# Column sums for norms: rows or squares added on VectorE and one product with ones per chunk

## The chip, the cores and the metric

The kernel runs on one core of a Trainium2 chip. The metric is the device time of one execution in microseconds. A core has TensorE (PE; its weight loads are shown apart as PEld), VectorE (DVE), ScalarE (ACT), GpSimd (POOL), SyncE (SP) and DMA queues. Each engine works through its instructions in order; they wait for each other by semaphores.

## What is computed

Two blocks of a transformer-like network, one after the other, on 1024 tokens of 1024 features (the first with 16 more meta tokens, the second with a context of 256 tokens beside). The change touches only the sums over features that the norms need. In short:

```
# block 1
h = concat(meta, x)
p = rmsnorm(h, g) @ w_in                    # state-space mixer (s5) and gated recurrence (hgrn)
merged = sigmoid(.) * (y_a @ w_a) + sigmoid(.) * (y_b @ w_b)
h = h + merged @ w_out
z = rmsnorm(h, ffn_norm_g)                  # "merge" ends with this norm
u = causal_dwconv(z @ w_up)
h = h + (silu(u1) * u2) @ w_down
x = rmsnorm(h, final_norm_g)                # "ffn" ends with this norm
# block 2, first mixer (ab), for the context and for x
ctx = layer_norm(ALPHA * ctx + gate_c * ab_mixer(ctx), g, b)      # "context path"
x   = layer_norm(ALPHA * x + gate * ab_mixer(x), g, b)            # "ab_x"
# block 2, second mixer (cd: Fourier mixing and attention)
x   = layer_norm(ALPHA * x + gate * cd_mixer(x, ctx), g, b)       # "cd"

rmsnorm(x)    = x * rsqrt(mean(x * x) + EPS) * g
layer_norm(x) = (x - mean(x)) * rsqrt(mean((x - mean(x))^2) + EPS) * g + b
```

## The kernel before

Features lie on partitions, tokens on columns. So an activation of 1024 features is eight row tiles of 128 partitions, and a sum over features is a sum over partitions and over eight tiles. Tokens are worked on in three chunks, of 384, 256 and 384 columns (384, 384 and 258 in merge, 256 alone in the context path). A weight product is exact in fp32 to the accuracy wanted: weights and activations are split into two parts, and `mm3` (line 83) issues three products for each 128 x 128 block. In ffn's down projection they are at line 949. In the trace such a product is one record; an fp32 product with ones, which goes through the array in two passes, is two.

A stage that ends in a norm is written with `closing` (line 754): the first panels (128 output features each) go through all chunks, the last `nres` (3 in merge, 6 in ab_x, 7 in cd) chunk by chunk, so that the norm of one chunk can run beside the weight products of the next. The rows of the first panels are added up in one tile `acc` on VectorE. For the last panels, the sum over partitions goes through TensorE. Merge (`sq=True`) issues full-width products with a matrix of ones (lines 779 and 792), accumulating in one bank. The others call `col_sum` (line 800): four sources at a time go through 32 columns of ones each, side by side in the array, into four groups of 32 output partitions (line 813); ScalarE copies the four partial sums out (line 817), and one more product with a selection matrix adds them up in every partition (line 818). `tail` sources skip this and go straight into that last bank (line 808).

`ln_chunk` (line 1038) is the layer norm of a chunk: mean (line 1042), centring of the eight rows (line 1045), squares on ScalarE (line 1047), their `col_sum`, `rsqrt` (lines 106 to 111), and `emit`, which scales the rows and makes the next stage's input. Ffn's last group of products (lines 957 to 965) squares each finished row on ScalarE (line 963) and sums with `col_sum`; then `x1_chunk` (line 977) norms. The context path (line 1221) sums eight rows, then calls `ln_chunk`.

The order of instructions on each engine isn't the order of the code: a scheduler of the framework places them by its own estimate when what they read is ready. Weight products' banks (`mm`) are four, banks of the sums (`sm`) four.

## Time and profile before

| | |
|---|---|
| time, median of 3 runs | 3249.68 us (3247.68 to 3250.23) |
| span of the profiled execution, first to last instruction | 3242.6 us |
| the profiled execution's own time | not listed apart; the median is 7.1 us above the span |
| mean granted TensorE clock | 0.995 |
| TensorE busy | 3165.4 us, 98% |
| VectorE busy | 1831.4 us, 56% |
| ScalarE busy | 1126.1 us, 35% |

Busy shares are means over the whole span. Where the kernel waits is read from the timelines of the engines, the windows (busy time of each engine in a stretch) and the waits. The five stages are found at about 966 to 979 us (context path), 1340 to 1392 (merge), 2096 to 2153 (ffn), 2451 to 2518 (ab_x) and 3130 to 3218 us (cd). In a timeline, consecutive instructions of one kind are one row; the square brackets hold the idle time before it and what ended that.

### The profile page before, as it was taken

How to read it: one execution, taken by the hardware profiler on the slowest of the kernel's cores; microseconds unless marked ns; L12 is line 12 of the kernel's file. 1: busy time of each engine (PE TensorE's matmuls, PEld its weight loads, DVE VectorE, ACT ScalarE, POOL GpSimd, SP SyncE). 2: the span in 40 equal slices, each digit the busy share in tenths (PEclk: the TensorE clock that was granted, in tenths of full speed). 3: DMA queues.
4: the chain of work that ended last, by engine and by line, in shares of the span. 5: the costliest groups of instructions: out<-in, count | busy, mean ns of one | idle time of the engine just before them, and what ended most of it. 6: DMA issues, size and time to landing. Idle time of an engine off the chain costs nothing.

```text
span 3242.6 us, 47786 instructions
## 1 busy us (share of the span) xinstructions
PE 3165.4 (98%) x19986; PEld 2840.8 (88%) x19986; DVE 1831.4 (56%) x3508; ACT 1126.1 (35%) x1846; POOL 92.9 (3%) x99
## 2 busy tenths in 40 slices
PE   8999899999999999999999999999999999999998
PEld 6999887879999999999999999989997889555476
DVE  7549468775454334465554555455336464777744
ACT  5341733233344312232222222252224353544532
POOL 0000000000210000000000000000000000121100
PEclk9999999999999999999999999999999999999999
DMA  4342454343552234111111111111111223000211
GB/s 153 90 161 91 148 182 142 118 153 103 158 155 81 91 118 130 33 59 46 40 46 53 47 52 40 53 35 54 46 40 66 92 88 130 29 7 7 79 49 52
DMA packets 106384, 269.01 MB, mean 83 GB/s; under 512 B 14798, under 2 KB 43694, under 8 KB 105974
## 3 DMA queue, kind: packets, MB, share of 16 engines
q1 hardware_dynamic: 99656, 245.35, 23.3%
q10 hardware_dynamic: 4464, 16.34, 1.3%
q0 software_dynamic: 2048, 4.26, 0.7%
q8 instruction: 157, 2.57, 0.3%
q14 instruction: 59, 0.48, 0.0%
HBM read 219.12 MB, written 46.11 MB: 82 GB/s over the span
## 4 chain that ended last, share of the span: by engine, by line
PE 90%; DVE 4%; DMA 2%; ACT 2%; issue 1%; SPq 0%; DVEq 0%; ACTq 0%
PE mm L83 62%; PE mm L949 7%; PE sm L1558 4%; PE mm L1555 4%; PE sm L813 2%; PE mm L1124 2%; PE sm L1531 1%; DMA YBd<-o 1%; PE mm L1516 1%; ACT Tt L502 1%; DVE R L604 1%; PE sm L465 1%; PE sm L1573 0%; PE sm L708 0%; PE sm L1017 0%
## 5 line engine op out<-in xcount | busy, mean ns | idle before, releaser
L83 PE MATMUL mm<-z,whl 128*128 128x256 f32 (+3 forms) x4032 | 682.9, 325 | 1.5 <-ACT z L231 1.0
L83 PE MATMUL mm<-a,whl 128*128 128x384 f32 (+1 forms) x4320 | 682.7, 319 | 1.6 <-ACT u L917 1.6
L83 PEld LDWEIGHTS mm<-a,whl 128*128 128x128 f32 x4320 | 678.5, 188 | 3.7 <-ACT u L917 1.9
L83 PEld LDWEIGHTS mm<-z,whl 128*128 128x128 f32 x4032 | 637.6, 189 | 36.8 <-issue 29.2
L76 DVE TENSOR_TENSOR whl<-wraw,whl 128x1024 fp32r<-128x1024 f32 (+2 forms) x258 | 302.6, 1178 | 221.1 <-ACT whl L75 220.3
L75 ACT CAST whl<-wraw 128x1024 fp32r<-128x1024 f32 (+2 forms) x258 | 260.6, 1014 | 341.8 <-PE mm L949 137.0
L83 PE MATMUL mm<-hx,whl 128*128 128x384 f32 (+1 forms) x2232 | 366.3, 322 | 7.7 <-ACT fx L1378 7.1
L83 PEld LDWEIGHTS mm<-hx,whl 128*128 128x128 f32 x2232 | 352.0, 189 | 16.8 <-ACT fx L1378 7.3
L949 PE MATMUL mm<-g,whl 128*128 128x384 f32 (+1 forms) x1584 | 257.9, 322 | 2.3 <-DVE f L951 1.2
L949 PEld LDWEIGHTS mm<-g,whl 128*128 128x128 f32 x1584 | 248.0, 188 | 13.9 <-issue 8.1
L83 PE MATMUL mm<-b,whl 128*128 128x384 f32 (+1 forms) x1152 | 180.9, 319 | 0.0
L83 PEld LDWEIGHTS mm<-b,whl 128*128 128x128 f32 x1152 | 180.8, 189 | 0.0
L917 ACT COPY u<-mm 128x384 f32<-128x384 f32 x132 | 58.3, 445 | 317.8 <-PE mm L83 317.8
L951 DVE TENSOR_TENSOR f<-f,mm 128x384 f32<-128x384 f32 (+1 forms) x240 | 118.3, 508 | 71.3 <-PE mm L949 70.4
L1556 ACT ACTIVATE P<-mm 128x512 f32<-128x512 f32 x160 | 94.7, 597 | 134.4 <-PE mm L1555 127.9
L83 PEld LDWEIGHTS mm<-y,whl 128*128 128x128 f32 x816 | 120.2, 188 | 13.1 <-issue 9.8
L83 PE MATMUL mm<-y,whl 128*128 128x256 f32 (+1 forms) x816 | 128.1, 312 | 1.4 <-ACT y L741 1.1
L1558 PE MATMUL sm<-P,m 128*64 128x512 f32 x320 | 128.0, 611 | 0.6 <-ACT P L1556 0.5
L1532 DVE TENSOR_REDUCE mx<-sm 128x1 f32<-128x512 f32 (+1 forms) x192 | 105.7, 595 | 39.7 <-PE sm L1531 38.4
L1555 PE MATMUL mm<-m,KB 97*128 97x512 f32 x420 | 121.7, 405 | 0.0
L1555 PEld LDWEIGHTS mm<-m,KB 97*128 97x128 f32 x420 | 75.6, 188 | 47.4 <-issue 33.3
L923 DVE TENSOR_SCALAR av<-u,conv_w,conv_b 128x1024 f32<-128x1024 f32 x22 | 17.9, 812 | 138.7 <-ACT u L917 138.7
(519 smaller groups left out, 3664.0 us busy)
## 6 DMA issues: line engine op xcount, KB each, us to landing
wraw<-w_up SPq DMA_DIRECT2D x44, 512.0 KB, 3.2
wraw<-w_h SPq DMA_DIRECT2D x32, 512.0 KB, 3.4
wraw<-ab_w SPq DMA_DIRECT2D x32, 512.0 KB, 3.4
wm<-ab_w_mod SPq DMA_DIRECT2D x24, 512.0 KB
wm<-cd_w_mod SPq DMA_DIRECT2D x24, 512.0 KB, 4.0
wraw<-w_down SPq DMA_DIRECT2D x22, 512.0 KB, 3.2
ut<-Ud SPq DMA_DIRECT2D x16, 520.0 KB, 4.5
gt<-Gd SPq DMA_DIRECT2D x16, 513.0 KB, 3.2
```

The lines of the kernel that those rows point to most:

```text
L75: self.nc.scalar.copy(t[:, 0], raw)
L76: self.nc.vector.tensor_tensor(out=t[:, 1], in0=raw, in1=t[:, 0].bitcast(F32), op=ALU.subtract)
L83: nc.tensor.matmul(ps, W[:, wp, wofs + 128 * k:wofs + 128 * k + 128], X(xp, kofs + k, lo, hi), start=first and k == 0 and i == 0, stop=las ...
L813: nc.tensor.matmul(p4[32 * j:32 * j + 32], self.ones[:, 0:32], x, start=i < 4, stop=i - len(pend) + j + 5 >= m)
L917: return u, (self.split_w(A["w_up"][p], [1024]), lambda c, lo, hi, ps: nc.scalar.copy(u[:, lo:hi], ps))
L949: nc.tensor.matmul(ps, ws[j][:, wp, 128 * o:128 * o + 128], G[j][:, xp, lo:hi], start=n_ == 0 and i == 0, stop=n_ == len(js) - 1 and i == 2)
L951: v.tensor_tensor(out=h1[o][:, 2 + lo:2 + hi], in0=h1[o][:, 2 + lo:2 + hi], in1=ps, op=ALU.add)
L1124: nc.tensor.matmul(ps, X(xp, k, 128 * t, 128 * t + 128), wv[k // 4][:, wp, 256 * (k % 4):256 * (k % 4) + 256], start=k == 0 and i == 0, st ...
L1532: v.tensor_reduce(out=mx[:, qt, j:j + 1], in_=ps, axis=mybir.AxisListType.X, op=ALU.max)
L1555: nc.tensor.matmul(ps, K[0:97, kp, 128 * t:128 * t + 128], Q[0:97, qp, 512 * c:512 * c + 512], start=i == 0, stop=i == 2)
L1556: nc.scalar.activation(Pt[:, c], ps, AF.Exp, scale=scale)
L1558: nc.tensor.matmul(po[64 * c:64 * c + 64, :], vv(t)[:, 64 * h:64 * h + 64], Pt[:, c], start=t == 0, stop=t == KT - 1)
```

## The change

In 18 of the 23 column sums, the eight rows (or squares) of a chunk are added up on VectorE and go through one full-width product with ones. `closing` adds the last panels' rows, or for merge their squares, to `acc` as well; in the last chunk the last row goes through a product of its own into the same bank. Ffn adds its squares in `tot` in the same manner. `ln_chunk` adds the squares in the tile of the first one, except in the last chunk of a closing (`tail` 1), where `col_sum` stays. The context path adds its eight rows in the first tile of `sqs`, whose other three tiles then take the squares in turn. The sums of the opening norm stay as they are. By the order of instructions TensorE has 122 products fewer (of 18548), VectorE 107 instructions more, ScalarE 15 fewer. Removed comments make up the rest of the diff and are left out here.

```diff
@@ closing
         for c, (lo, hi) in enumerate(chunks):
             n = hi - lo
-            if sq:
-                pc = self.ps_sm()[:, 0:n]
-                nc.tensor.matmul(pc, self.ones, acc[:, lo:hi], start=True, stop=False)
-            else:
-                add = self.col_sum(nres + 1, n, lambda: tp.tile([128, 384], F32, tag="mu", name=self.nm("cse"), bufs=1), int(hi == chunks[-1][1]))
-                add(0, acc[:, lo:hi])
             for j, (w, o) in enumerate(ws):
...
                 if sq:
                     t = tp.tile([128, 384], F32, tag="tmp", name=self.nm("sqt"), bufs=2)[:, 0:n]
                     nc.scalar.activation(t, src, AF.Square)
-                    nc.tensor.matmul(pc, self.ones, t, start=False, stop=i == npan - 1)
-                else:
-                    pc = add(j + 1, src)
+                    src = t
+                if i == npan - 1 and hi == chunks[-1][1]:
+                    nc.tensor.matmul(pc, self.ones, src, start=False, stop=True)
+                    continue
+                nc.vector.tensor_tensor(out=acc[:, lo:hi], in0=acc[:, lo:hi], in1=src, op=ALU.add)
+                if i == npan - (2 if hi == chunks[-1][1] else 1):
+                    pc = self.ps_sm()[:, 0:n]
+                    nc.tensor.matmul(pc, self.ones, acc[:, lo:hi], start=True, stop=i == npan - 1)
             done(c, lo, hi, pc)
@@ ffn, last group
-                    add = self.col_sum(8, n, lambda: tp.tile([128, 384], F32, tag="cse", name=self.nm("cse"), bufs=1), int(c == 2))
+                    tot = tp.tile([128, 384], F32, tag="cse", name=self.nm("cse"), bufs=1)[:, 0:n]
                     for o in range(8):
                         one(o, lo, hi)
-                        t = tp.tile([128, 384], F32, tag="tmp", name=self.nm("sqt"), bufs=6)[:, 0:n]
+                        t = tp.tile([128, 384], F32, tag="tmp", name=self.nm("sqt"), bufs=6)[:, 0:n] if o else tot
                         nc.scalar.activation(t, h1[o][:, 2 + lo:2 + hi], AF.Square)
-                        pc = add(o, t)
+                        if o == 7 and c == 2:
+                            nc.tensor.matmul(pc, self.ones, t, start=False, stop=True)
+                            continue
+                        if o:
+                            v.tensor_tensor(out=tot, in0=tot, in1=t, op=ALU.add)
+                        if o == (6 if c == 2 else 7):
+                            pc = self.ps_sm()[:, 0:n]
+                            nc.tensor.matmul(pc, self.ones, tot, start=True, stop=o == 7)
@@ ln_chunk
-        add = self.col_sum(8, n, lambda: tp.tile([128, 384], F32, tag="mu", name=self.nm("cse"), bufs=1), tail)
+        if tail:
+            add = self.col_sum(8, n, lambda: tp.tile([128, 384], F32, tag="mu", name=self.nm("cse"), bufs=1), tail)
         for k in range(8):
             v.tensor_tensor(out=r(k), in0=r(k), in1=mu, op=ALU.subtract)
             t = sqt(k)[:, 0:n]
             nc.scalar.activation(t, r(k), AF.Square)
-            ps = add(k, t)
+            if tail:
+                ps = add(k, t)
+            elif k == 0:
+                t0 = t
+            else:
+                v.tensor_tensor(out=t0, in0=t0, in1=t, op=ALU.add)
+        if not tail:
+            ps = self.ps_sm()[:, 0:n]
+            nc.tensor.matmul(ps, self.ones, t0, start=True, stop=True)
@@ ctx_path
-            add = self.col_sum(8, T, lambda: tp.tile([128, 384], F32, tag="mu", name=self.nm("cse"), bufs=1))
-            for k in range(8):
-                ps = add(k, x[:, k])
             sqs = cp.tile([128, 4, T], F32, name="csq")
-            self.ln_chunk(tp, lambda k: x[:, k], ps, T, emit, lambda k: sqs[:, k % 4], 0)
+            tot = sqs[:, 0]
+            v.tensor_tensor(out=tot, in0=x[:, 0], in1=x[:, 1], op=ALU.add)
+            for k in range(2, 8):
+                v.tensor_tensor(out=tot, in0=tot, in1=x[:, k], op=ALU.add)
+            ps = self.ps_sm()[:, 0:T]
+            nc.tensor.matmul(ps, self.ones, tot, start=True, stop=True)
+            self.ln_chunk(tp, lambda k: x[:, k], ps, T, emit, lambda k: sqs[:, 1 + (k - 1) % 3 if k else 0], 0)
```

The order of instructions that results is shown at three places. The names are the output tile and what it is computed from, with the output's shape; x3 stands for three in a row.

TensorE, before, at the end of ffn's third chunk: `g` with `whl` are its weight products, `sqt` with `ones` the squares, `hx` the input of the next stage.

```order
L813 MATMUL sm_19587<-sqt_19671,ones 32x384
L813 MATMUL sm_19587<-sqt_19687,ones 32x384
L949 MATMUL mm_19711<-g_18997,whl_19191 128x384
L813 MATMUL sm_19587<-sqt_19703,ones 32x384
L949 MATMUL mm_19711<-g_18997,whl_19191 128x384
L949 MATMUL mm_19711<-g_19178,whl_19196 128x384 x3
L83 MATMUL mm_19808<-hx_19351,whl_19803 128x384 x2
L83 MATMUL mm_19834<-hx_19351,whl_19803 128x256
L818 MATMUL sm_19588<-cse_19708,sel 128x384
L83 MATMUL mm_19834<-hx_19351,whl_19803 128x256
L83 MATMUL mm_19808<-hx_19351,whl_19803 128x384
L808 MATMUL sm_19588<-sqt_19725,ones 128x384
```

TensorE, after, at the same place (`cse` is now the tile of the added squares):

```order
L950 MATMUL mm_19691<-g_18606,whl_19178 128x384 x3
L950 MATMUL mm_19691<-g_18989,whl_19183 128x384 x3
L950 MATMUL mm_19691<-g_19170,whl_19188 128x384 x3
L83 MATMUL mm_19788<-hx_19339,whl_19783 128x384
L972 MATMUL sm_19689<-cse_19571,ones 128x384
L966 MATMUL sm_19689<-sqt_19705,ones 128x384
L83 MATMUL mm_19788<-hx_19339,whl_19783 128x384 x2
L83 MATMUL mm_19788<-hx_19340,whl_19783 128x384 x3
```

Before, the narrow products of the squares stand among the weight products of the last rows; after, the two full products stand together, behind the last weight product and one product of the next stage.

VectorE, before, the layer norm of ab_x's first chunk, from the fifth centring on: `f` are the rows, `mu` the mean, L1309 adds products of the second chunk.

```order
L1045 TENSOR_TENSOR f_12897<-f_12897,mu_22537 128x384
L1045 TENSOR_TENSOR f_13003<-f_13003,mu_22537 128x384
L1045 TENSOR_TENSOR f_13034<-f_13034,mu_22537 128x384
L1045 TENSOR_TENSOR f_13065<-f_13065,mu_22537 128x384
L1309 SCALAR_TENSOR_TENSOR f_12709<-mm_22625,mod_ab,f_12709 128x256
L1309 SCALAR_TENSOR_TENSOR f_12803<-mm_22639,mod_ab,f_12803 128x256
```

VectorE, after, from the third centring on (`sqt` are the squares):

```order
L1054 TENSOR_TENSOR f_12701<-f_12701,mu_22513 128x384
L1054 TENSOR_TENSOR f_12795<-f_12795,mu_22513 128x384
L1062 TENSOR_TENSOR sqt_22516<-sqt_22516 128x384
L1054 TENSOR_TENSOR f_12889<-f_12889,mu_22513 128x384
L1062 TENSOR_TENSOR sqt_22516<-sqt_22516,sqt_22522 128x384
L1054 TENSOR_TENSOR f_12993<-f_12993,mu_22513 128x384
```

The adds of the squares stand between the centrings, one behind each from the fourth row on.

TensorE, before, the squares of ab_x's first chunk among the weight products (`y` with `whl`) of the second:

```order
L83 MATMUL mm_22639<-y_22094,whl_22415 128x256 x3
L83 MATMUL mm_22639<-y_22288,whl_22415 128x256
L813 MATMUL sm_22539<-sqt_22542,ones 32x384 x2
L83 MATMUL mm_22639<-y_22288,whl_22415 128x256 x2
L813 MATMUL sm_22539<-sqt_22547,ones 32x384
L83 MATMUL mm_22653<-y_21429,whl_22421 128x256 x3
L813 MATMUL sm_22539<-sqt_22547,ones 32x384
L83 MATMUL mm_22653<-y_21623,whl_22421 128x256 x3
L83 MATMUL mm_22653<-y_22094,whl_22421 128x256
L813 MATMUL sm_22539<-sqt_22556,ones 32x384 x2
L83 MATMUL mm_22653<-y_22094,whl_22421 128x256 x2
```

TensorE, after, the sum of the same squares:

```order
L83 MATMUL mm_22670<-y_22074,whl_22407 128x256 x3
L83 MATMUL mm_22670<-y_22268,whl_22407 128x256 x2
L1065 MATMUL sm_22542<-sqt_22516,ones 128x384
L83 MATMUL mm_22670<-y_22268,whl_22407 128x256
L83 MATMUL mm_22769<-y_21409,whl_22395 128x384 x3
L83 MATMUL mm_22769<-y_21603,whl_22395 128x384 x3
```

The eight narrow products, of which six are shown, became one full product, which stands at the end of the second chunk's weight products.

## Rows read from the trace of the kernel before

**Rows 1.** The page, sections 1 and 4: TensorE's share, and the chain that ended last.

```profile
PE 3165.4 (98%) x19986; PEld 2840.8 (88%) x19986; DVE 1831.4 (56%) x3508; ACT 1126.1 (35%) x1846; POOL 92.9 (3%) x99
...
PE 90%; DVE 4%; DMA 2%; ACT 2%; issue 1%; SPq 0%; DVEq 0%; ACTq 0%
```

**Rows 2.** Narrow products (L813) by stage: window, its length, PE busy, PEld busy, PEclk, DMA.

```profile
966.00:979.00 13.00, 5.32 (x32) 1.51 (x32) 1.00 0.07 28
...
2096.00:2153.00 57.00, 12.67 (x46) 2.51 (x46) 1.00 0.03 9
2451.00:2518.00 67.00, 19.46 (x86) 3.77 (x86) 1.00 0.19 66
3130.00:3218.00 88.00, 18.67 (x78) 3.65 (x78) 1.00 0.09 31
```

**Rows 3.** PE's timeline in cd: start us, us, engine, line, out<-in, shape, records.

```profile
3200.19 0.52 PE L813 MATMUL sm<-m,ones 128*32 128x384 f32 x2
...
3200.96 0.44 PE L83 MATMUL mm<-yc,whl 128*128 128x384 f32 x1
3201.34 0.83 PE L813 MATMUL sm<-m,ones 128*32 128x384 f32 x2
3202.10 1.14 PE L83 MATMUL mm<-yc,whl 128*128 128x384 f32 x5
...
3217.43 0.81 PE L818 MATMUL sm<-cse,sel 128*128 128x384 f32 x2
3217.79 1.68 PE L83 MATMUL mm<-yc,whl 128*128 128x384 f32 x7
```

**Rows 4.** PE's timeline in ab_x: the first of five runs of narrow products.

```profile
2509.98 0.84 PE L813 MATMUL sm<-sqt,ones 128*32 128x384 f32 x4
```

**Rows 5.** Merge's products of squares (L792) and what PE waited for before them (us, times).

```profile
L792 PE MATMUL sm<-sqt,ones x18: 381/486/590, 1347.1 to 1391.4; 128*128 128x384 f32 x12, 128*128 128x258 f32 x6
...
  ACT sqt L791: 1.7, 7
```

**Rows 6.** VectorE's timeline: eight centrings (L1045) of 384 and of 256 columns.

```profile
2464.59 3.84 DVE L1045 TENSOR_TENSOR f<-f,mu 128x384 f32<-128x384 f32 x8
...
3183.87 2.77 DVE L1045 TENSOR_TENSOR m<-m,mu 128x256 f32<-128x256 f32 x8
```

**Rows 7.** Busy time by engine in three stretches: length, PE, PEld, DVE, ACT, POOL, PEclk.

```profile
2464.00:2512.00 48.00, 48.00 (x266) 34.09 (x265) 37.09 (x82) 30.87 (x66) 0.00 (x0) 1.00 0.23 78
...
3130.00:3218.00 88.00, 88.00 (x507) 69.18 (x505) 28.89 (x61) 18.72 (x40) 0.00 (x0) 1.00 0.09 31
1375.00:1390.00 15.00, 15.00 (x103) 14.88 (x102) 14.64 (x26) 7.91 (x14) 0.00 (x0) 1.00 0.32 106
```

**Rows 8.** Timelines of ScalarE (four rows) and VectorE (last row) around the norms.

```profile
979.26 0.47 ACT L106 ACTIVATE rsy<-sm,eps 128x256 f32<-128x256 f32 x1
...
1391.78 0.48 ACT L106 ACTIVATE rsy<-sm,eps 128x258 f32<-128x258 f32 x1 [0.79 <-PE sm L792]
...
2142.63 3.00 ACT L963 ACTIVATE sqt<-f 128x384 f32<-128x384 f32 x7
...
2518.00 0.58 ACT L106 ACTIVATE rsy<-sm,eps 128x384 f32<-128x384 f32 x1 [1.77 <-PE sm L808]
...
2509.72 1.49 DVE L1045 TENSOR_TENSOR f<-f,mu 128x384 f32<-128x384 f32 x3
```

**Rows 9.** PE's timeline at three places, then two windows by engine with PEclk (before DMA).

```profile
1401.07 11.24 PE L83 MATMUL mm<-a,whl 128*128 128x258 f32 x78 [1.61 <-ACT u L917]
...
2150.07 0.63 PE L83 MATMUL mm<-hx,whl 128*128 128x384 f32 x3
...
2529.71 6.49 PE L83 MATMUL mm<-hx,whl 128*128 128x256 f32 x34 [7.11 <-ACT fx L1378]
...
2528.00:2532.00 4.00, 2.29 (x10) 2.29 (x11) 2.21 (x7) 3.79 (x7) 0.00 (x0) 0.50 0.93 267
2532.00:2536.00 4.00, 4.00 (x25) 4.00 (x25) 0.58 (x2) 1.16 (x4) 0.00 (x0) 0.67 0.35 113
```

## The prediction, made before the changed kernel had run

> **What bounds the kernel now.** The page comes first: TensorE is busy 98% of a span of 3242.6 us, and the chain that ended last is TensorE for 90% [rows 1]. So a microsecond taken from TensorE counts, unless something else is then late. The median of the runs, 3249.68 us, is 7.1 us above this span; those 7.1 us lie outside the first and last instruction, so I work in the span and take the difference off the median.
>
> Next, what a column sum costs TensorE now. In the five stages the narrow products (32 of the array's columns) are busy 5.32, 12.67, 19.46 and 18.67 us (context, ffn, ab_x, cd); merge has none [rows 2]. The timeline shows why so much: three narrow sources side by side keep the next weight product away from 3200.19 to 3200.96. After one weight product comes a single source, and the next weight product is at 3202.10: 1.14 us, of which a weight product of 384 columns takes .18, so .96 went to one source. A full-width fp32 product with ones (two passes) holds TensorE .36 us: 3217.43 to 3217.79 [rows 3]. The narrow form costs two to three times a full product, however many sources lie side by side, and the sources come one or two at a time.
>
> By the Trainium skill, "TensorEngine Tiling (Array Packing)", section "Theoretical Speedup", a dimension of at most 32 gives up to 4 times the speed, so narrow products side by side would be the cheap form. Its section "Tiling Modes", under Key Properties, says that a change of tiling mode drains the engine; the .96 us for one source agrees with that clause, not with the speedup.
>
> **The change part by part.** 18 sums change: 2 in the context path, 3 in merge, 3 in ffn, 5 in ab_x, 5 in cd. Left alone are the three at the kernel's opening and the squares of the last chunk in ab_x and in cd.
>
> *TensorE.* In each changed sum the gathering product (.36) is replaced by the product of ones with the added rows (.36), so what is freed is the narrow products. Context: 5.3. Ffn: 12.7. Cd: 18.7. Ab_x: 19.46 less the five runs that stay (the first at 2509.98, .84 us [rows 4]; 4.2 together) = 15.3. Merge has full products already: 12 become 4, 8 x .36 = 2.9, and the 1.7 us in which those products waited for their squares [rows 5] can go too: 4.6. Sum: 56.6 us. That is the upper end.
>
> *VectorE.* It gets 107 adds, 57 of 384 columns and 50 of 256 or 258. The nearest rows are the centrings, which also take two rows and give one: 3.84/8 = .48 us and 2.77/8 = .35 us [rows 6]. So 57 x .48 + 50 x .35 = 44.9 us on an engine busy 56% [rows 1]. What matters is where they fall.
>
> *Cd* (34 adds, 20 x .48 + 14 x .35 = 14.5 us). VectorE is busy 28.9 of 88.0 us [rows 7]; with the adds 43.4, still under TensorE's 88 - 18.7 = 69. Each chunk's squares must be centred, squared, added and summed before TensorE reaches the product. For the first chunk the chain is 15 x .48 (eight centrings, seven adds) and about 2.3 us for the mean, the last square and the hops between engines, which I put at five adds' worth: 9.5 us. Ahead of the product I count 72 weight products of 256 columns, at two thirds of .18 each 8.6 us: a wait of about 1 us, and as little in the second chunk (39 products of 384, 7.0 us, against 15 x .35 + 2.3 = 7.6). Gain 18.7 - 1 = 18 in round numbers (16 to 19). The tail after 3218 is unchanged.
>
> *Ffn* (20 adds). The third chunk's squares start at 2142.63 on ScalarE, behind the second chunk's norm on the same queue [rows 8]. In the new order one product of the next stage stands between the third chunk's last weight product and its sum. That stage starts at 2150.07 now [rows 9]; with nearly all of the 12.7 us gone, TensorE would be there at about 2137. The first and second sum come 4 and 5 us earlier (four or five narrow runs of .96), and so does the second norm: ScalarE begins the squares at about 2137.6, takes 3.0 us for seven of them [rows 8], and the last add follows: 2141. TensorE waits about 4 us, and all products of the next mixer are queued behind that. 12.7 - 4 = 9 (6 to 12; the low end has half clock behind the wait).
>
> *Ab_x* (31 adds, 13.2 us). From 2464 to 2512 VectorE is busy 37.1 of 48 us [rows 7], and 10.3 us of the adds fall there (12 x .48 + 13 x .35): 47.4, full. TensorE's 15 us therefore can't all be taken: VectorE sets the pace. The first chunk's sum comes 2.9 us earlier (three narrow runs of .96 fewer), so the window starts near 2461 and the last centred row, which ends now at 2511.2 [rows 8], ends near 2507.5. Its seven narrow squares then go to TensorE in about one block, not in five, and the norm's root is at about 2511 where it is at 2518.00 [rows 8]. The products that wait 7.11 us before 2529.71 [rows 9] hang on that norm, and so start 7 us earlier. They wait less than before, since TensorE's freed time is spent in earlier waits. After the 7.11 us the granted clock is .50 and then .67 [rows 9], that is the lower of its two levels until about 2534.6: 4.9 us at half speed, 2.45 lost. With a shorter last wait these come back: 7 + 2 = 9 (5 to 12).
>
> *Merge* (8 adds). The third norm's root stands at 1391.78 [rows 8]; VectorE is busy 14.64 of the 15 us before 1390 [rows 7], so the third chunk's row comes hardly earlier, 1.2 us at most, and TensorE then waits longer at 1401.07 (1.61 now [rows 9]; 1.6 + 4.6 - 1.2 = 5). A wait of 5 us may bring the half clock: -2.4. Gain 0 (-2 to 4).
>
> *Context* (14 adds of 256). The mean is ready at about the same time, since 15 x .35 of adds and centrings take the place of scattered products. The root, at 979.26 now [rows 8], comes some 2 us earlier and the keys' products wait for it. Gain 2 (0 to 5).
>
> *Edits with no cost of their own.* 15 copies of the four partial sums leave ScalarE, off the path. SyncE's queue has a few weight loads a place earlier or later; no changed stretch shows TensorE waiting for a load, so 0. With that cover gone it would be one wait like those in [rows 9].
>
> Sum: 18 + 9 + 9 + 0 + 2 = 38 us, 3249.7 - 38 = 3212. The lows make 25, the highs 52: 3198 to 3225.
>
> **The rivals.**
>
> *TensorE alone counts.* No new wait ends late; 56.6 us come off: 3193. For it: 98% busy. Against: ab_x's VectorE has no room [rows 7], and waits for ScalarE stand there already [rows 9].
>
> *Waits twice as long.* Each add stands in one in-order queue behind whatever VectorE does, the product in another behind it; if the waits in cd, ffn and ab_x (1, 4 and 15.3 - 7 = 8 us) are double what I reckon, 38 becomes 25, and half clock behind one to seven of them (2.45 apiece) leaves 8 to 23: about 3233. For it: merge's squares kept TensorE waiting seven times [rows 5] though VectorE wasn't in that path.
>
> *The sources side by side cost the time of one.* This is a mechanism by which nothing is gained: a sum of eight sources would hold TensorE 2 x .36 for its two groups and .36 for gathering, against .36, so .7 x 15 = 11 us (merge has no such sums) would come free, and the 13 us of new waits above take them: no change, 3249. [rows 3] speaks against it: one source alone took .96. By the Trainium skill, "TensorEngine Tiling (Array Packing)", section "Theoretical Speedup", this is what side by side should do.
>
> *Slower: the sum holds the queue.* The product with ones stands in TensorE's in-order queue before weight products that don't need it. If the scheduler puts it as soon as its rows are out, TensorE stands for the whole chain of adds: 44.9 us over all sums, and 2.45 of half clock behind each of 18: 44.9 + 44.1 - 56.6 = 32 us slower, 3281. It decides from 56.6 / 18 = 3.1 us of wait per sum. For it: in ffn's last chunk the product stands right behind the rows. Against: elsewhere dozens of weight products stand between.
>
> **How the numbers follow.** Forecast .71; TensorE alone .07; waits doubled .14; side by side as one .04; slower .04. 0.2% is 6.5 us, about what a measurement can tell from none. Faster is the first three, .92; same .04; slower .04. Predicted is the forecast's 3212. The range takes the forecast's own 3198 to 3225, down to 3193 for TensorE alone and up to 3232 for about half of the doubled waits: .71 + .07 + .06, a little over 8 in 10.
>
> **What would show it.** TensorE's records fall by 244 (122 products of two passes) and the narrow products from 304 records to 76; VectorE's instructions rise by 107. Right, step by step: cd from its first sum to 3218 is some 18 us shorter with no wait over 1.5 us before a sum; ffn shows one wait of about 4 us before its third sum; in ab_x VectorE has next to no idle from the first centring to the last, and the products after the norm start some 18 us earlier, counted with the 11 gained before it, with full clock; merge's wait at 1401 grows to about 5 us. Wrong: waits before sums in cd (its adds not hidden), or in ab_x an unchanged wait of 7 us before the products after the norm, or half clock behind waits where I have none. If TensorE's busy time falls by much less than 56 us, the price of a narrow product was mistaken.

## The result, and the profile after

The changed kernel took 3211.04 us (3205.94 to 3212.52, 4 runs) beside 3248.68 us (4 runs) for the kernel before: ratio 0.9889, 95% interval 0.9875 to 0.9903, 37.6 us faster. The forecast was 3212. The span of its profiled execution is 3208.4 us, 34.2 less than before's. In every run listed with its span the time is about 1.8 us above the span, so the profiled execution of the kernel before took some 3244.4 us, one of the faster ones.

The page: TensorE's busy time fell by 56.4 us (forecast 56.6), its records by 244, the narrow ones from 304 to 76, and VectorE's instructions rose by 107, all as foreseen. The agreement of the busy time is in part chance: the mean granted clock fell from .995 to .992, and products at half clock are busy longer. Then the chain that ended last, in which TensorE has 87% where it had 90% [rows 1].

```profile
PE 3109.0 (97%) x19742; PEld 2832.6 (88%) x19742; DVE 1878.1 (59%) x3615; ACT 1119.5 (35%) x1831; POOL 93.1 (3%) x99
...
PE 87%; DVE 6%; ACT 4%; DMA 3%; issue 1%; SPq 0%; ACTq 0%; DVEq 0%
```

TensorE's other products are the same in both kernels and stand in nearly the same order (19544 records). So the start of the n-th one in either trace tells how far ahead the changed kernel is at that point, and the difference between two points is what a stage gave (cd is counted to the end of the span). This is worked out from the records, not a view of the profile:

| stretch | forecast | first trace | second trace of the same kernel |
|---|---|---|---|
| ahead of the context path (unchanged) | 0 | -2.7 | -0.4 |
| context path | 2 (0 to 5) | 1.1 | 0.9 |
| merge | 0 (-2 to 4) | 0.0 | -1.3 |
| ffn | 9 (6 to 12) | 6.6 | 8.2 |
| ab_x | 9 (5 to 12) | 9.7 | 9.7 |
| between ab_x and cd (unchanged) | 0 | -1.2 | -1.2 |
| cd | 18 (16 to 19) | 20.9 | 20.9 |
| the five stages together | 38 | 38.3 | 38.4 |

The second trace is that of `e10_after_again`, below. The 2.7 us that the first one lost early on, where no sum was changed, were 0.4 in the second: chance between runs (over all traces of this study it was from 4.5 lost to .2 gained). The five stages sum to the forecast in both, but not by its terms.

**Cd.** TensorE's timeline around the two sums of squares (start, duration, engine, line, out<-in, shape, records; in brackets idle time and what ended it): no bracket, so no wait. A sum is one row, where [rows 3] shows narrow products in between.

```profile
3143.55 1.58 PE L83 MATMUL mm<-yc,whl 128*128 128x256 f32 x12
...
3145.20 0.88 PE L1065 MATMUL sm<-m,ones 128*128 128x384 f32 x2
3145.62 1.89 PE L83 MATMUL mm<-yd,whl 128*128 128x256 f32 x12
...
3162.71 2.09 PE L83 MATMUL mm<-yd,whl 128*128 128x384 f32 x11
...
3164.74 0.67 PE L1065 MATMUL sm<-m,ones 128*128 128x256 f32 x2
3165.06 0.53 PE L83 MATMUL mm<-yd,whl 128*128 128x384 f32 x1
```

**Ffn.** TensorE stands 4.43 us at the first product of the next stage, and behind it are the sum (L972) and the last row's square (L966). ScalarE's timeline: the seven squares, 2.4 us later than foreseen (1.7 of them were lost before this stage), and behind them the cast of the next stage's weights, which ends the wait. VectorE's adds end at 2144.64, 1.6 us behind the last square: six adds into one tile, one behind the other, take 3.87 us and start .66 us apart; in ab_x's first norm, where they alternate with centrings, each instruction starts .47 behind the one before. In the second trace (last row) the sum waits for them another .26 us. The window behind the wait (PE, PEld, DVE, ACT, POOL busy, then PEclk) is at half clock.

```profile
2144.00 0.69 PE L83 MATMUL mm<-hx,whl 128*128 128x384 f32 x1 [4.43 <-ACT whl L75]
...
2144.69 1.65 PE L972 MATMUL sm<-cse,ones 128*128 128x384 f32 x2
2146.13 1.49 PE L966 MATMUL sm<-sqt,ones 128*128 128x384 f32 x2
...
2140.02 2.99 ACT L964 ACTIVATE sqt<-f 128x384 f32<-128x384 f32 x7
2142.92 1.97 ACT L75 CAST whl<-wraw 128x1024 fp32r<-128x1024 f32 x2
...
2140.77 3.87 DVE L969 TENSOR_TENSOR cse<-cse,sqt 128x384 f32<-128x384 f32 x6
...
2142.30 1.58 PE L972 MATMUL sm<-cse,ones 128*128 128x384 f32 x2 [0.26 <-DVE cse L969]
```
```profile
2144.00:2148.00 4.00, 4.00 (x7) 2.38 (x8) 2.83 (x3) 1.24 (x2) 0.00 (x0) 0.50 0.12 26
```

**Ab_x.** Four waits of TensorE before the norm of the last chunk, and 1.91 us behind it where [rows 9] had 7.11. The windows show VectorE busy 43.76 of 44 us, and half clock behind the second wait and again behind the fourth. The last centred row ends at 2500.09, and the root of the last chunk's norm is at 2505.65 (2518.00 in [rows 8]).

```profile
2463.33 1.52 PE L83 MATMUL mm<-y,whl 128*128 128x256 f32 x11 [1.61 <-DVE f L1329]
...
2482.39 4.11 PE L83 MATMUL mm<-y,whl 128*128 128x384 f32 x12 [5.86 <-DVE f L1329]
...
2488.42 0.91 PE L795 MATMUL sm<-aacc,ones 128*128 128x384 f32 x2 [0.80 <-DVE aacc L792]
...
2498.84 3.97 PE L814 MATMUL sm<-sqt,ones 128*32 128x384 f32 x14 [4.83 <-ACT sqt L1056]
...
2517.36 12.81 PE L83 MATMUL mm<-hx,whl 128*128 128x256 f32 x87 [1.91 <-ACT fx L1398]
```
```profile
2456.00:2500.00 44.00, 30.90 (x174) 27.94 (x173) 43.76 (x105) 27.05 (x58) 0.00 (x0) 0.88 0.21 72
...
2482.00:2486.00 4.00, 3.61 (x11) 3.61 (x12) 4.00 (x11) 0.93 (x1) 0.00 (x0) 0.50 0.01 2
...
2498.00:2502.00 4.00, 3.16 (x14) 1.28 (x14) 3.23 (x7) 4.00 (x11) 0.00 (x0) 0.50 0.00 0
```
```profile
2499.06 1.03 DVE L1054 TENSOR_TENSOR f<-f,mu 128x384 f32<-128x384 f32 x2
...
2505.65 0.58 ACT L106 ACTIVATE rsy<-sm,eps 128x384 f32<-128x384 f32 x1 [2.33 <-PE sm L809]
```

**Merge.** The wait at the next stage's products is 5.05 us (1.61 in [rows 9]), and the window behind it has a granted clock of .60.

```profile
1401.33 13.94 PE L83 MATMUL mm<-a,whl 128*128 128x258 f32 x86 [5.05 <-ACT u L918]
```
```profile
1400.00:1404.00 4.00, 2.67 (x12) 2.67 (x13) 1.29 (x4) 2.32 (x6) 0.00 (x0) 0.60 0.00 0
```

### The profile page after: what moved, and what is told of

It is laid out like the page before. It is cut to its first block, busy times and chain, and to the rows that moved or that the text cites. A ratio compares the mean times of both kernels' runs of the same rounds, so it can differ in the third digit from the quotient of the medians.

```text
span 3208.4 us, 47429 instructions
## 1 busy us (share of the span) xinstructions
PE 3109.0 (97%) x19742; PEld 2832.6 (88%) x19742; DVE 1878.1 (59%) x3615; ACT 1119.5 (35%) x1831; POOL 93.1 (3%) x99
## 4 chain that ended last, share of the span: by engine, by line
PE 87%; DVE 6%; ACT 4%; DMA 3%; issue 1%; SPq 0%; ACTq 0%; DVEq 0%
PE mm L83 61%; PE mm L950 7%; PE mm L1575 4%; PE sm L1578 4%; PE mm L1141 2%; DMA YBd<-o 1%; PE sm L1551 1%; PE mm L1536 1%; DVE R L604 1%; ACT Tt L502 1%; PE sm L465 1%; DVE B L599 1%; PE sm L1593 0%; PE sm L708 0%; PE sm L814 0%
## 5 line engine op out<-in xcount | busy, mean ns | idle before, releaser
L1552 DVE TENSOR_REDUCE mx<-sm 128x1 f32<-128x512 f32 (+1 forms) x192 | 105.7, 596 | 39.7 <-PE sm L1551 38.4
```

The costliest lines, as they stand in the source:

```text
L1552: v.tensor_reduce(out=mx[:, qt, j:j + 1], in_=ps, axis=mybir.AxisListType.X, op=ALU.max)
```

## The experiments

In all of them the sums that aren't named stay as in the kernel that is named as the base. Stage gains are read as in the table above, against the trace of the kernel before.

**What a full product costs, without adds.** Base: the kernel before.

```diff
 def add(i, src):          # in col_sum, for all sums but the opening's
+    if self.n > self.n0:  # behind the opening
+        nc.tensor.matmul(ps, self.ones, src, start=i == 0, stop=i == ns - 1)
+        return ps
```

By this edit the squares of the last chunk of ab_x and of cd, which the change leaves narrow, go through full products as well.

> The kernel before, but every source of the changed sums goes through a full-width product with ones (128 columns) into one bank: no narrow products, no copy and gathering product, and no adds on VectorE either. Theory (a narrow run costs .8 to 1.0 us because TensorE changes its tiling, however many sources it holds): by the rows of before, 56 us of narrow products and 5 us of gathering products go, and about 120 full products at .36 (384 columns) or .24 us (256) come, 37 us: 24 us of TensorE time freed, of which new waits eat some: 12 to 26 us faster than before, 3223 to 3237. Rival (what counts is the number of products, not their width): as many products as before, so no change within 4 us. Second rival (TensorE's time isn't what ends last in ab_x and merge): ab_x keeps its wait of 7 us before the products behind the norm, and ab_x gains under 3 us.

3230.07 us beside 3243.91 for the kernel before, ratio 0.9957 (0.9940 to 0.9973): about 14 us faster, inside the theory's range, but not by its prices. By stages: context 1.2, merge 1.9 (its sums are as before; its wait of 1.61 us is gone, and why is not shown), ffn 3.5, ab_x 9.1, cd -0.7. In cd, the narrow products were exchanged for full ones and nothing was won (.4 up to the last weight product; 1.1 were lost behind it, where the last squares are eight full products). The timeline shows the price: from one panel's start to the next, 3113.42 to 3118.38, are 4.96 us, for 24 weight products of .175 each (4.20) and a single full product.

```profile
3113.42 1.02 PE L84 MATMUL mm<-yc,whl 128*128 128x384 f32 x5
3114.29 0.91 PE L834 MATMUL sm<-m,ones 128*128 128x384 f32 x2
3114.75 1.67 PE L84 MATMUL mm<-yc,whl 128*128 128x384 f32 x7
...
3118.38 1.03 PE L84 MATMUL mm<-yc,whl 128*128 128x384 f32 x5
```

So the full product costs .76 us here, not the .36 that I had read from [rows 3]. Ab_x gained as much as in the changed kernel, by another way: its products before the norm give TensorE no less to do, but the norm of the last chunk has no copy and no gathering product behind the squares, and the products behind it wait .33 us:

```profile
2517.70 17.54 PE L84 MATMUL mm<-hx,whl 128*128 128x256 f32 x114 [0.33 <-ACT fx L1419]
```

**The price by itself.** Base: the changed kernel. The probes add zeros to the panel's own bank; the sums and outputs stay what they are.

```diff
 for k in range(nk):        # mm3, called from cd's closing
+    if probe and k == 4:
+        kind, z = probe
+        for g in range({"A": 1, "B": 4, "D": 8}.get(kind, 0)):
+            nc.tensor.matmul(ps[32 * (g % 4):32 * (g % 4) + 32], self.ones[:, 0:32], z, start=False, stop=False)
+        for g in range({"C": 1, "E": 4}.get(kind, 0)):
+            nc.tensor.matmul(ps, self.ones, z, start=False, stop=False)
...
+probe=("CABECDB"[j], zt[:, 0:n])     # kind by panel
```

> The changed kernel with a probe in the middle of each of the seven last panels of each cd chunk, a product with ones of a source of zeros into the panel's own bank, so that the scheduler can't move it: kinds by panel are one full product, one narrow, four narrow side by side, four full, one full, eight narrow, four narrow. Read from the starts of the weight products around each. Theory (change of tiling): 384 columns: one full .36 us, four full 1.44, one narrow .9 to 1.0, four narrow the same .9 to 1.1, eight narrow 1.2 to 1.5. Rival (each product costs by itself): four narrow 3 to 4 times one narrow. Second rival (one narrow costs no more than one full, and the .96 us of the rows were waits for data): one narrow .36 to .45.

A single run, whose time isn't used. TensorE's timeline in cd's first chunk. The distance from one `yc` row to the next `yc` row behind a probe holds 24 weight products (in the changed kernel 4.21, from 3167.51 to 3171.72) and the probe.

```profile
3111.05 2.24 PE L89 MATMUL mm<-yc,whl 128*128 128x384 f32 x12
3113.22 0.83 PE L85 MATMUL mm<-zt,ones 128*32 128x384 f32 x2
...
3116.21 2.24 PE L89 MATMUL mm<-yc,whl 128*128 128x384 f32 x12
3118.38 0.85 PE L85 MATMUL mm<-zt,ones 128*32 128x384 f32 x8
...
3121.39 2.26 PE L89 MATMUL mm<-yc,whl 128*128 128x384 f32 x12
3123.49 2.74 PE L87 MATMUL mm<-zt,ones 128*128 128x384 f32 x8
...
3128.15 2.26 PE L89 MATMUL mm<-yc,whl 128*128 128x384 f32 x12
3130.25 0.81 PE L87 MATMUL mm<-zt,ones 128*128 128x384 f32 x2
...
3132.99 2.26 PE L89 MATMUL mm<-yc,whl 128*128 128x384 f32 x12
3135.18 1.50 PE L85 MATMUL mm<-zt,ones 128*32 128x384 f32 x16
...
3138.80 2.26 PE L89 MATMUL mm<-yc,whl 128*128 128x384 f32 x12
```
```profile
3167.51 2.28 PE L83 MATMUL mm<-yd,whl 128*128 128x384 f32 x12
...
3171.72 2.27 PE L83 MATMUL mm<-yd,whl 128*128 128x384 f32 x12
```

| probe, 384 columns | distance | less 4.20 | 256 columns |
|---|---|---|---|
| one narrow | 5.16 | .96 | .74 |
| four narrow, side by side | 5.18 | .98 | .77 |
| eight narrow | 5.81 | 1.61 | 1.20 |
| one full | 4.84 | .64 | .43 |
| four full | 6.76 | 2.56 | 1.73 |

The distances with 256 columns are taken less 2.84 in the same way; in front of its four full products stands a sum, whose .29 us are off too.

The narrow prices came out as the theory had them, so both rivals fall: four sources cost what one costs, and one costs more than a full product. The full price did not: .64, and four of them four times that. A full product is two records (the two passes of the texts above), which start .32 us apart, where a weight product of the same columns is one record and takes .175; so the two take .64. In `e1_full` it was .76: where VectorE has only just made the row, the second record comes .43 us behind the first and not .32; why is not shown. The weight product behind it starts early and is drawn out, which is why the distance of two starts right at the product, as I read it in [rows 3], shows only .36. The drawn-out row was there: 7 weight products last 1.68 us from 3217.79, and by a row of 12 that no sum precedes (2.26 above) it would be 2.26 - 5 x .175 = 1.39, so .29 of the full product's time lay in it.

By the Trainium skill, "TensorEngine Tiling (Array Packing)", section "Theoretical Speedup", narrow products gain up to 4 times; four sources at .98 against 2.56 are 2.6 times, and one source alone loses. Over a full product for each four sources, the narrow form costs .32 to .34 us, once per run; that agrees with the clause in section "Tiling Modes", under Key Properties, that a change of tiling mode drains the engine. No run here shows the draining apart.

**Cd alone.** Base: the kernel before; `closing` and `ln_chunk` take the changed branch only when they are called from `cd_close`.

```diff
 for c, (lo, hi) in enumerate(chunks):
+    if sq or nk == 4:
+        ...
+        continue
...
+        cs = tail or self.where in ("ab", "ctx")
+        if cs:
+            add = self.col_sum(8, n, ..., tail)
```

> The kernel before with the five sums of the cd stage alone changed. Theory (in cd nothing ends late but TensorE, its adds are hidden): 18 to 21 us faster than before, 3228 to 3231. Rival (the 20.9 us that the two traces differ by in cd are partly the drift between runs, the stage itself gives 12 to 15): 3234 to 3237.

3222.22 us beside 3243.91, ratio 0.9934 (0.9919 to 0.9949), 21.7 us by the medians and 20.8 by the aligned trace. The rival of a drift is out: cd gave 20.6 to 20.9 in the traces in which it was changed and that have no probes, but one (18.9, `e8_ffn_c2_full`). There it gave 20.8 up to the last weight product; the other 2 us were lost behind it, in the last norm, whose products ran at a granted clock of .50.

**All but ab_x.** Base: the changed kernel, with the old branch where `nk == 4` and, in `ln_chunk`, where it is called from ab_x.

```diff
 for c, (lo, hi) in enumerate(chunks):
+    if nk == 4:
+        ...
+        continue
...
+        cs = tail or self.where == 'ab'
```

> The changed kernel with ab_x's five sums as before. Theory (ab_x's part gave 9.6 us by the two traces, though VectorE is full there): 3220 to 3222, 9 to 11 us slower than the changed kernel. Rival (where VectorE sets the pace the adds return what TensorE gained, and the stage gave 0 to 4 us): 3211 to 3215.

3216.68 us, ratio 0.9913 (0.9898 to 0.9928). By the ratio to the kernel before that is 8 us slower than the changed kernel (.9889; each of the two ratios has an interval of 5 us to either side); by the aligned trace ab_x gave -.3, 10 us less than the 9.7 of the changed kernel. The rival, 0 to 4, doesn't hold. In this trace ffn gave 8.2 and merge -1.3, as in the second trace of the changed kernel: in the two traces of the changed kernel the waits there are of the same length (4.43 and 5.05 us), and what differs is how long the half clock lasts behind them.

**The adds on another engine.** Base: the changed kernel.

```diff
-                v.tensor_tensor(out=t0, in0=t0, in1=t, op=ALU.add)
+                (nc.gpsimd if self.where == 'ab' else v).tensor_tensor(out=t0, in0=t0, in1=t, op=ALU.add)
```

> The changed kernel with the 14 adds of squares in ab_x's first two layer norms on GpSimd instead of VectorE. Theory (VectorE is full from the first centring to the last in ab_x and sets the pace): 5.9 us leave VectorE's queue; of the 13 us that TensorE waits there (1.6, 5.9, .8, 4.8) 2 to 5 go, 2 to 5 us faster than the changed kernel. Rival (GpSimd's adds are slow, about 1 us each as its 99 instructions of 93 us, and the sum comes later): the first chunk's sum comes 3 us later than now and TensorE waits at it, 2 to 6 us slower.

3224.82 us, ratio 0.9934 (0.9919 to 0.9948), where the changed kernel has .9889; ab_x lost 3.8 us against the kernel before, 13.5 against the changed kernel: the rival's way, and twice its size. GpSimd takes 1.22 us for an add of 384 columns in a row of six, and the sum's product, in TensorE's queue ahead of weight products that don't need it, holds them up for 5.27 us in the first chunk and 5.00 in the second:

```profile
2462.07 7.31 POOL L1063 TENSOR_TENSOR sqt<-sqt,sqt 128x384 f32<-128x384 f32 x6
...
2469.44 1.65 PE L1066 MATMUL sm<-sqt,ones 128*128 128x384 f32 x2 [5.27 <-POOL sqt L1063]
...
2494.67 1.22 PE L1066 MATMUL sm<-sqt,ones 128*128 128x256 f32 x2 [5.00 <-POOL sqt L1063]
```

This is the rival "the sum holds the queue" of the prediction, made to happen by a slower chain: from 3.1 us of wait per sum it was to decide, and in this stage it did.

**Ab_x's squares by full products, in the last chunk or in all.** Base: the changed kernel. For all chunks `full = self.where == 'ab'`, for the last `full = tail and self.where == 'ab'`.

```diff
+        if full:
+            ps = self.ps_sm()[:, 0:n]
-        if tail:
+        elif tail:
             add = self.col_sum(8, n, ..., tail)
...
+            if full:
+                nc.tensor.matmul(ps, self.ones, t, start=k == 0, stop=k == 7)
-            if tail:
+            elif tail:
                 ps = add(k, t)
```

> The changed kernel; only the squares of ab_x's last chunk, which it left as narrow products with a copy and a gathering product behind, go through eight full products into one bank. Theory (the norm of that chunk is what the next stage waits for, and the copy and gathering stand between): in the full-product run the root came 2.8 us after the last centred row, in the changed kernel 5.6; so root 2.7 us earlier, the wait of 1.9 us before the products behind it gone: 2 to 3 us faster than the changed kernel, 3208 to 3209.5 on its scale. Rival (eight full products of .65 us take what the narrow block of 4.0 us took and more): no change within 1 us.

3212.55 us, ratio 0.9893 (0.9878 to 0.9907): no faster; ab_x gave 8.6 in the aligned trace, 1.1 less than in the changed kernel. The rival holds. The eight products start behind the same wait of 4.83 us and run at half clock for more than half of their time (.50 from 2502 to 2506), 7.70 us for the block where the narrow one took 3.97:

```profile
2501.85 7.70 PE L1062 MATMUL sm<-sqt,ones 128*128 128x384 f32 x16 [4.83 <-ACT sqt L1060]
```

> The changed kernel with ab_x's layer norms of all three chunks by eight full products each and no adds of squares there (its closing sums stay added up). VectorE loses 14 adds, 5.9 us; TensorE gets 7 x .65 + 7 x .43 = 7.6 us more. Theory (VectorE sets the pace in ab_x, TensorE has 15 us of waits and 5 us of half clock there): 3 to 6 us faster than the changed kernel. Rival (TensorE's queue holds the eight products in a block until the last square, so the wait only moves): within 1.5 us of the last-chunk-only version.

3208.58 us, ratio 0.9884 (0.9870 to 0.9899). The medians can't tell it from the changed kernel; in the aligned trace ab_x gave 12.4, 2.7 more than the changed kernel (a little under the theory's 3 to 6) and 3.8 more than the last-chunk-only version (the rival had 1.5 at most). The theory's mechanism shows in the windows: the same stretch has VectorE at 40.78 of 44 us, TensorE at 39.38 where it was 30.90, and a granted clock of .99 where it was .88. VectorE, which waited .2 us in that stretch, now waits 3.8 us for TensorE's products. How much of the 2.7 us is room on VectorE and how much the clock, this run doesn't tell apart. The waits of 1.61 and 5.86 us are gone, the one at the last chunk's squares is left:

```profile
2456.00:2500.00 44.00, 39.38 (x216) 34.00 (x215) 40.78 (x94) 28.02 (x60) 0.00 (x0) 0.99 0.21 72
```
```profile
2498.00 7.12 PE L1062 MATMUL sm<-sqt,ones 128*128 128x384 f32 x16 [4.02 <-ACT sqt L1060]
```

**Ffn's third chunk by full products.** Base: the changed kernel.

```diff
-                        if o == 7 and c == 2:
-                            nc.tensor.matmul(pc, self.ones, t, start=False, stop=True)
+                        if c == 2:
+                            if o == 0:
+                                pc = self.ps_sm()[:, 0:n]
+                            nc.tensor.matmul(pc, self.ones, t, start=o == 0, stop=o == 7)
                             continue
...
-                        if o == (6 if c == 2 else 7):
+                        if o == 7:
```

> The changed kernel; only the squares of ffn's third chunk go through eight full products as they come, without adds. Theory (the 4.4 us wait there and the half clock behind it are why ffn gave 6.6 and not 9): TensorE works on the squares from about 2141 while the weights of the next stage are still cast, the wait falls to about 1 us and the half clock goes: 2 to 3.5 us faster than the changed kernel. Rival (the wait is for the weights' cast on ScalarE, which stands behind the squares, and has nothing to do with the sum): TensorE has its products later and resumes the next stage no earlier, within 1 us or slower.

3211.48 us, ratio 0.9896 (0.9878 to 0.9913), nothing to be told from the medians; in the aligned trace ffn gave 8.9, 2.3 more than in the first trace of the changed kernel and .7 more than in the second. The rival is right that the cast of the weights is a limit too, the next stage starting at 2145.13. But TensorE starts on the squares after .18 us, is busy with them until the cast is done, and goes on with the next stage at full clock (its timeline, then the window by engine with PEclk):

```profile
2140.80 4.78 PE L968 MATMUL sm<-sqt,ones 128*128 128x384 f32 x14 [0.18 <-ACT sqt L964]
2145.13 5.13 PE L83 MATMUL mm<-hx,whl 128*128 128x384 f32 x28
```
```profile
2144.00:2148.00 4.00, 4.00 (x20) 3.34 (x20) 3.73 (x5) 1.99 (x4) 0.00 (x0) 1.00 0.18 40
```

**Both, beside the changed kernel again.** Base: the changed kernel with the edit of ffn above, and `full = not tail and self.where == 'ab'`.

> The changed kernel with two sums by full products instead of adds: the squares of ab_x's first two chunks and those of ffn's third chunk; ab_x's last chunk stays narrow. Theory (the two changes act on waits of two stages and add up: 2.3 us in ffn, 2.7 to 3.8 us in ab_x by the traces): 5 to 6 us faster than the changed kernel run beside it. Rival (half clock or another wait of the same chain takes one of them back): 2 to 3 us.

> The changed kernel once more, beside the one above, as its scale on this chip. Theory (its gain is 37 to 38 us, and the 2 to 4 us of drift ahead of the context path in the first trace are chance between runs): ratio .987 to .990 to the kernel before, and a drift in this trace that need not be the same.

3204.08 us (ratio 0.9869, 0.9853 to 0.9886) and 3209.31 us (0.9886, 0.9871 to 0.9901) on the same chip: 5.2 us by the medians, with intervals that overlap. The aligned traces have ab_x at 13.2 (9.7) and ffn at 8.9 (8.2), together 4.2 us more, between the theory's 5 to 6 and the rival's 2 to 3, and neither is ruled out. It has the lowest median of this study, 44.6 us ahead of the kernel before. The changed kernel came out again as expected, and its loss ahead of the context path was .4 this time.

## Why the prediction was right, and where its terms were not

The total, 38 us, and the order of the stages held; three terms were off and cancelled, which is luck. The prediction also took 7.1 us for time outside the first and last instruction; by the runs with a span that is 1.8 us, and the rest was the difference between the profiled execution and the median. The forecast, taken off the median, doesn't hang on it.

- **Cd, 18 forecast, 20.9 measured, above its own range.** The mechanism was right: no wait over 1 us, the adds hidden. The term that failed is the size of what is freed: I took the busy time of the narrow records (18.67), and not what a run takes away from the weight products. In cd 24 runs stood among them, 14 of 384 and 10 of 256 columns: with the prices of the probe 14 x .97 + 10 x .76 = 21.2. And the wait of about 1 us that I took off did not come.
- **The price of a full product, .36 forecast, .64 measured.** It entered nearly nowhere, since each gathering product was exchanged for one product with ones. Where it did enter, in merge, the chain of the norm decided anyway. In `e1_full` it decides: at .36 and .24 the 39 products that took the place of cd's narrow runs and of five gathering products (23 of 384, 16 of 256 columns) would have cost 12 us; at .64 and .43 they cost 22, and 2 more where the second record was late, as much as the 21 of the runs and 3 of the gathering products that they replaced.
- **Ffn, 9 forecast, 6.6 and 8.2 measured, within its range.** The wait of 4 us was right (4.43), and so was its cause, ScalarE's squares behind the second norm. The last link was not as I had it: I let the last add follow the last square, and it came 1.6 us behind, since adds into one tile start .66 us apart and not .48; and the cast of the next stage's weights, behind the squares on ScalarE, ended the wait nearly as late as the sum would have. The rest is half clock, which I had put into the low end only. `e8_ffn_c2_full` gave back .7 to 2.3 us, by which of the two traces it is set against.
- **Ab_x, 9 forecast, 9.7 measured.** VectorE full (43.76 of 44 us), the stage 7.5 us ahead at the products behind the norm (4.89 ahead at its start, 12.35 there; forecast 7), the last wait down from 7.11 to 1.91 with full clock behind it, and 2.2 us for that clock: as forecast. Two misses cancelled inside it. Counted from the stage's start, the last centred row came 2.5 us earlier than forecast, but the root 5.6 us behind it and not 3.5: the narrow squares ran at half clock, and six weight products of the next stage stood between them and the gathering product. Half clock behind two of the earlier waits (5.86 and 4.83) is what I had named as a sign of being wrong. The products behind the norm start 12.35 us earlier and not 18: the stages before had given 4.89 and not 11. That VectorE set the pace is shown by its busy time and by the waits, three of the four for its rows and sums, and `e7_abx_ln_full` fits it: with 5.9 us of adds taken off it, and 7 us of products put on TensorE, the stage became 2.7 us shorter.
- **Merge, 0 forecast, 0.0 and -1.3 measured.** The wait grew to 5.05 us, forecast 5, with half clock behind it.
- **Context, 2 forecast, 1.1 and 0.9 measured.** The sums are off TensorE, but two new waits of 1.9 and 1.5 us stand behind the norm, and between them TensorE follows the rows as ScalarE delivers them (1.6 us more), so most was given back.

Of the rivals, "TensorE alone counts" fell by the waits in ffn, ab_x and merge; "waits twice as long" by their length, which was as forecast (none in cd, 4.43 in ffn, and in ab_x 13.1 before the norm less the 5.2 that the wait behind it lost, 7.9 against 8); "the sources side by side cost the time of one" is true of four sources in one run (.98 against .96), but the kernel before issued them in cd one to three at a time, so what was paid was 24 runs and not the 10 that the code groups them in. "The sum holds the queue" was no part of this change and is what `e6_pool` shows.

Open: why 1.1 to 1.5 us are lost between ab_x and cd in four traces of kernels with ab_x as changed, and not in a fifth (`e8_ffn_c2_full`), and what sets how long the half clock lasts behind a wait of the same length. The loss lies at two places, by the times of the kernel before at 2658 us (.4 to 1.1; in the second trace half of it is a wait for ScalarE's cast of weights) and at 3053 us (0 to 1.1, a wait for ScalarE's `P` in the attention); why these come late is not shown.

## What to carry to other kernels

An extra product in a stream of weight products is priced by the distance of the same panel points with and without it, not by the distance of two starts beside it. Narrow products side by side are worth having when four sources really go out together; one at a time they cost more than full ones, and adding the rows up on an engine with time to spare beats both. Where that engine has no time to spare, or the adds stand one behind the other at the end of a chain, full products may be better: here they gave some 3 us more in ab_x and .7 to 2.3 in ffn by the traces, too little for the medians to confirm. Decide stage by stage.

## What the runs showed of the hardware

- An fp32 product with ones of 384 columns took .64 us of TensorE's time in a stream of weight products of .175 us (`e4_probe`), in two records .32 apart, and .76 in `e1_full`, where its row had only just been made.
- Four narrow fp32 products of 384 columns side by side took .98 us, one alone .96, eight 1.61 (`e4_probe`).
- VectorE's adds of 384 columns took .47 us from start to start when they alternated with centrings, and .66 when six in a row went into one tile (3.87 us, changed kernel); GpSimd's six took 7.31 us, 1.22 each (`e6_pool`).
